# Down projections of three layers turned to stationary tokens and Strassen's scheme, with norm roots on GpSimd

## The chip, the cores and the metric

The kernel runs on one core of one Trainium2 chip. The metric is the time of one execution on the device in microseconds (us). All multiplications are done on TensorE in products of 128 x 128 stationary values against up to 512 moving columns; VectorE, ScalarE and GpSimd (POOL in the profile) prepare operands and read results, SyncE (SP) issues the transfers.

## The reference

A decoder trunk of four layers over one residual stream of 256 tokens with 1024 features. Layer i has the token mixer i mod 3: differential attention, block-sparse attention, sliding-window attention with sinks. Each layer ends in a squared-ReLU MLP with 4096 hidden features; a final norm follows. All in float32.

```python
def rms_norm(x, g):
    y = xf * lax.rsqrt(jnp.mean(xf * xf, axis=-1, keepdims=True) + NORM_EPS)
    return (y * g.astype(jnp.float32)).astype(x.dtype)

def sqrelu_mlp(h, w_up, w_down):
    a = jnp.maximum(h @ w_up, 0)
    return (a * a) @ w_down

for i in range(DEPTH):
    a = rms_norm(h, attn_norm_g[i])
    ...
    h = h + y
    h = h + sqrelu_mlp(rms_norm(h, mlp_norm_g[i]), mlp_w_up[i], mlp_w_down[i])
return rms_norm(h, final_norm_g)
```

## The kernel before

**Precision.** Each operand is split into a high part in the fast format fp32r and a low remainder; a product is the sum of three TensorE products (high x high, high x low, low x high). Weights come in pieces of 128 x 2048 floats (1 MB, tile raw): ScalarE writes whi, VectorE subtracts and writes wlo, both in two halves of 1024 columns. There are four raw buffers and three pairs of whi and wlo.

**Residual stream.** It lies in hT0 to hT3 with features on partitions and tokens on columns. A norm multiplies its gain in first: `Normed.part` writes hg, high part on ScalarE and low part on VectorE, which is the operand of the next products. The norm's scale is put in after the products. `Normed.sum` adds up squares in acc; `row` sums acc over partitions with a GpSimd all-reduce (tile rows); `column` picks each token's sum onto its partition with VectorE (tile nx); `factor` takes the inverse root (tile nr) by ten small VectorE steps, except in layer 0, where the sums come by products and GpSimd's power takes the root. The evictions of the mixer's first products p_in (tile qk, or vkq in layer 2) multiply by nr. After them come the rotation (ropea, ropeb), the transposes p_qk and the scores p_s.

**MLP.** `up_proj` makes 4096 hidden features in 16 groups g of 256, with features on partitions: u is the squared ReLU, uu its high and low parts. The MLP norm's scale is the square of a root, so it's a reciprocal without a root, and it comes behind the down projection. In layers 0 to 2 `down_proj` holds the weights stationary: 8 blocks d of 128 output features, each with 32 blocks of hidden features, a 512-column product with whi (uu's high and low parts side by side) and a 256-column one with wlo, 512 in all. Each pair of blocks is evicted (cross, y), scaled by a row of factors and added to hT.

In layer 3 `down_out` holds the tokens stationary (uu's 128 tokens) and streams 512 output features of the weights. The first 1024 hidden features (g 0 to 3) go by Strassen's scheme with a Winograd form: tokens, hidden features and output features are each halved, and seven products of sums replace eight. `Sums` makes the sums of u in `up_proj`, `Form` and `less` the sums of the weights. Seven `strassen` steps of 4 x 3 products and twelve `plain` pieces of 24 follow one another; results gather in PSUM banks (sums, products p, p_last, p_end), `shared` adds what Strassen's products share. There the result has tokens on partitions, as the output wants it.

**Order.** `Plan` places all tasks: a list scheduler runs a model of the engines forth and back, with a cost written beside each task, and keeps the best of eight orders; EARLIER moves single tasks by hand, by their number (plan.named). The order of instructions on each engine's queue is then fixed, and each queue runs in order: an instruction that waits holds up all behind it.

Of the kernel before, what the change touches and what calls it, by code (L numbers as in the profile page):

```python
# [11 lines left out]
F32 = mybir.dt.float32  # L12
# [31 lines left out]
           4306: -5.2, 4309: -1.1, 4443: -7.1, 6437: -126, 6439: -126}  # L44
# [171 lines left out]
def trunk(ctx: ExitStack, tc: tile.TileContext, xT, gains, lams, swa_row, fng, weights, out):  # L216
# [291 lines left out]
    def rsqrt(y, x, n):  # L508

        t = tiny.tile([P, n], F32, tag="nw", name="nw", bufs=6)  # L510
        V.tensor_scalar(y.bitcast(I32), x.bitcast(I32), -0.5, 1597463007.0, op0=OP.mult, op1=OP.add)
        for _ in range(3):
            V.tensor_tensor(t, y, y, op=OP.mult)
            V.scalar_tensor_tensor(t, t, -0.5, x, op0=OP.mult, op1=OP.mult)
            V.scalar_tensor_tensor(y, t, 1.5, y, op0=OP.add, op1=OP.mult)

    norms = iter(range(100))

    class Normed:
# [704 lines left out]
    def up_proj(n, then, forms=None):  # L1224

        us, pair, read, done, used = [], {}, [None, None], [], {}
        for g in range(16):
# [40 lines left out]
            if forms is not None and g < 4:  # L1268
# [17 lines left out]

    def down_proj(us, n, row):

        def into(j, p, last, begin):

            st = {}

            def to():
                st["y"] = sb.tile([P, 512], F32, tag="y", name="y")
                return r3(2)(st["y"])

            def scaled():
                V.tensor_tensor(r3(2)(st["y"]), r3(2)(st["y"]), row[0][:, None, :].to_broadcast([P, 2, S]), op=OP.mult)
                V.tensor_tensor(hT[j], st["y"], hT[j], op=OP.add)

            a = joined(to, p, [last])
            s = dve(1024, scaled, [a, row[1]], 0.2)
            n.part(2 * j, [s])
            n.part(2 * j + 1, [s])
            n.sum(j, [s])
            give("acc", [a], begin)

        for d in range(8):
            if d % 2 == 0:
                st = {}  # L1310
            for h in range(2):
                w = piece()
                for part, k in ((part, k) for part in ((0, 1), (1, 0))[h] for k in range(16)):

                    def do(d=d, h=h, k=k, part=part, w=w, st=st):
                        if not st:
                            st["p"] = two_banks("p_down")
                        block_step(st["p"][:, d % 2], w.at(part, 16, k), us[16 * h + k][1](), part,
                                   h + k + part == 0, h == 1 and part == 0 and k == 15)

                    at = d % 2 + h + k + part
                    t = product(STEPS[part], do, [us[16 * h + k][0], w.ready(part, 16, k)], {"acc": 1} if at == 0 else None)
                    begin = t if at == 0 else begin
                release(w)
            if d % 2:
                into(d // 2, lambda st=st: st["p"], t, begin)
# [26 lines left out]
    def down_out(us, factor, forms):  # L1353

        st = {}
        res = stream_by_tokens()
        ss = cst.tile([P, NT, 4], F32, name="fss")
        x = cst.tile([P, NT], F32, name="fx")
        r = cst.tile([P, NT], F32, name="fr")
        last = []  # L1360

        def load():
# [355 lines left out]
```

## Time and profile before

| | us |
|---|---|
| median of 3 runs | 1121.19 (1121.08 to 1121.8) |
| the profiled execution's own time | 1121.43 |
| its span, first to last instruction | 1119.3 |
| TensorE busy | 1111.6 (99%) |
| VectorE busy | 845.1 (75%) |
| ScalarE busy | 695.8 (62%) |
| GpSimd busy | 62.7 (6%) |

Rows of the profile read thus: a chain's row is start, duration, engine and tile; a timeline's row is start, duration, engine, operation, output tile, arrow, inputs, and in brackets the idle time ahead of it with what ended it. Almost every instruction carries line 209, that of the helper which issues it, so tiles are named instead. PE is TensorE, PEld its weight loads, DVE VectorE, ACT ScalarE.

### The profile page before, as it was taken

To read this page: it belongs to the slowest core of one execution; us is meant where nothing else is said; L and a number is where in the kernel's file an instruction comes from. 1 tells how busy PE (TensorE), PEld (TensorE's weight loads), DVE (VectorE), ACT (ScalarE), POOL (GpSimd) and SP (SyncE) were. 2 spreads that over 40 slices of the span, in tenths; PEclk is the share of its full clock that TensorE was granted. 3 is DMA by queue.
4 is the path that set the end of the run, shared out by engine and by line. 5 is a ranking of instruction groups with operands and counts; after the bars stand their busy time and mean duration, and the time that the engine had idled before them with its cause. 6 is when DMAs were issued, how large, how long until landed. Compare 5 with 4: busy or idle time off the path is not lost.

```text
span 1119.3 us, 16680 instructions
## 1 busy us (share of the span) xinstructions
PE 1111.6 (99%) x6438; PEld 974.2 (87%) x6438; DVE 845.1 (75%) x1406; ACT 695.8 (62%) x1231; POOL 62.7 (6%) x109
## 2 busy tenths in 40 slices
PE   9999999999999999999999999999999999999997
PEld 7889888888888898888888898888888889888886
DVE  6996987646697678775569898865568787988847
ACT  6996655444497765554357965554448785655693
POOL 4110000000100000000001100000010110000000
PEclk9999999999999999999999999999999999999999
DMA  9545455555444455555553265555544445553740
GB/s 326 174 151 189 173 201 184 196 188 189 150 153 149 155 184 199 177 204 177 206 191 118 76 253 195 181 195 188 189 151 141 172 146 194 188 193 114 282 172 37
DMA packets 30462, 198.63 MB, mean 177 GB/s; under 512 B 3504, under 2 KB 4784, under 8 KB 7216
## 3 DMA queue, kind: packets, MB, share of 16 engines
q1 hardware_dynamic: 30096, 197.35, 50.3%
q8 instruction: 50, 0.82, 0.3%
q10 hardware_dynamic: 288, 0.23, 0.1%
q14 instruction: 28, 0.23, 0.1%
HBM read 196.52 MB, written 1.05 MB: 177 GB/s over the span
## 4 chain that ended last, share of the span: by engine, by line
PE 99%; DMA 0%; DVE 0%; issue 0%; POOL 0%; POOLq 0%; ACT 0%; SPq 0%; DVEq 0%
PE p_up L209 32%; PE p_down L209 24%; PE p_in L209 20%; PE p_d L209 8%; PE p_last L209 4%; PE p L209 3%; PE p_s L209 2%; PE p_av L209 2%; PE p_t L209 1%; PE p_qk L209 1%; PE p_o L209 0%; DMA hT<-in_xT 0%; DVE res L209 0%; POOL fr L209 0%; POOLq L1714 0%
## 5 line engine op out<-in xcount | busy, mean ns | idle before, releaser
L209 DVE TENSOR_TENSOR wlo<-raw,whi 128x1024 fp32r<-128x1024 f32 (+1 forms) x382 | 449.7, 1210 | 187.7 <-ACT whi L209 182.8
L209 ACT ACTIVATE whi<-raw 128x1024 fp32r<-128x1024 f32 (+1 forms) x382 | 380.1, 1038 | 221.1 <-issue 80.0
L209 PE MATMUL p_up<-hg,whi 128*128 128x512 f32 x1024 | 239.9, 390 | 0.0
L209 PEld LDWEIGHTS p_up<-hg,whi 128*128 128x128 f32 x1024 | 189.5, 188 | 38.1 <-DVE hg L209 0.6
L209 PE MATMUL p_in<-whi,hg 128*128 128x512 f32 (+1 forms) x672 | 187.7, 393 | 0.4 <-DVE hg L209 0.4
L209 PE MATMUL p_down<-uu,whi 128*128 128x512 f32 x768 | 179.1, 390 | 0.0
L209 PEld LDWEIGHTS p_down<-uu,whi 128*128 128x128 f32 x768 | 142.7, 188 | 28.6
L209 PEld LDWEIGHTS p_in<-whi,hg 128*128 128x128 f32 x672 | 122.2, 189 | 23.2 <-ACT whi L209 0.9
L209 PEld LDWEIGHTS p_up<-hg,wlo 128*128 128x128 f32 x1024 | 127.6, 192 | 2.8
L209 PE MATMUL p_up<-hg,wlo 128*128 128x256 f32 x1024 | 128.5, 283 | 0.0
L209 PE MATMUL p_in<-wlo,hg 128*128 128x512 f32 (+1 forms) x336 | 106.2, 393 | 0.0
L209 PEld LDWEIGHTS p_down<-uu,wlo 128*128 128x128 f32 x768 | 95.3, 192 | 1.9
L209 PE MATMUL p_down<-uu,wlo 128*128 128x256 f32 x768 | 95.9, 283 | 0.0
L209 PE MATMUL p_d<-oo,whi 128*128 128x256 f32 x512 | 94.9, 286 | 0.0
L209 ACT ACTIVATE uu<-u 128x512 fp32r<-128x512 f32 (+1 forms) x64 | 39.7, 620 | 79.5 <-DVE u L209 79.5
L209 PEld LDWEIGHTS p_d<-oo,whi 128*128 128x128 f32 x512 | 79.6, 191 | 1.1 <-issue 0.9
L209 PE MATMUL p_d<-oo,wlo 128*128 128x256 f32 x256 | 72.4, 283 | 0.0
L209 PEld LDWEIGHTS p_in<-wlo,hg 128*128 128x128 f32 x336 | 61.8, 189 | 11.8 <-DVE wlo L209 0.4
L209 ACT ACTIVATE e<-ns,nm 128x128 f32<-128x128 f32 (+3 forms) x128 | 56.9, 447 | 4.9 <-DVE nm L209 3.8
L209 ACT ACTIVATE cross<-p_up 128x512 f32<-128x512 f32 x64 | 37.7, 590 | 34.6 <-PE p_up L209 34.5
L209 DVE TENSOR_TENSOR relu<-p_up,cross 128x512 f32<-128x512 f32 x64 | 44.0, 688 | 14.0 <-ACT cross L209 13.9
L209 DVE TENSOR_TENSOR uu<-u,uu 128x512 fp32r<-128x512 f32 (+1 forms) x64 | 43.5, 680 | 13.3 <-ACT uu L209 12.6
(200 smaller groups left out, 1110.9 us busy)
## 6 DMA issues: line engine op xcount, KB each, us to landing
raw<-in_weights SPq DMA_DIRECT2D x181, 1024.0 KB, 4.9
raw<-in_weights SPq DMA_DIRECT2D x12, 256.0 KB, 5.0
hT<-in_xT SPq DMA_DIRECT2D x8, 128.0 KB, 4.4
raw<-in_weights SPq DMA_DIRECT2D x2, 512.0 KB, 6.7
bias<-in_swa_row SPq DMA_DIRECT2D x1, 512.0 KB, 6.8
grow<-in_fng SPq DMA_DIRECT2D x1, 512.0 KB, 5.3
out<-last SPq DMA_DIRECT2D x1, 512.0 KB, 2.7
out<-last SPq DMA_DIRECT2D x1, 320.0 KB, 2.6
```

Source lines behind the costliest of these rows:

```text
L209: x = getattr(self.engine, name)(*args, **kw)
```

## The change

The down projections of layers 0 to 2 now take the same path as that of layer 3 (`down_out` becomes `down_proj` for all), with the tokens stationary and Strassen's scheme on the hidden groups g 0 to 3. `up_proj` makes the sums in all layers, the weights are laid out accordingly (16 pieces per layer as before), and the MLP norm's factor is a column (a value per token on its partition) in place of a row. Since the residual stream of these layers has features on partitions, the result is turned back: y0 and y1 take the scaled results, one tile for each half of the tokens; the new function `back` mixes the banks in (mixed), transposes 128 x 128 blocks on TensorE into a bank p_y (turned_back) and adds these to hT (added), for each half c of the output features. The last bank is taken in two halves. `rsqrt` goes, and GpSimd's power takes the root of all mixer norms. The numbers of the tasks are set at each layer's start, so that EARLIER names the tasks it did.

The core of the diff (left out: the bodies of the removed functions, the weight layout, tile declarations, hand-overs of names):

```diff
-           4306: -5.2, 4309: -1.1, 4443: -7.1, 6437: -126, 6439: -126}
+           4306: -5.2, 4309: -1.1, 4443: -7.1, 6439: -126, 6441: -126}
...
-    def rsqrt(y, x, n):
...
         def factor(self, by_products):
             x, a = self.column_by_products() if by_products else self.column()
-            if by_products:
-                return add("POOL", 0.8, lambda: G.tensor_tensor(self.r, x, minus_half[:, :NT], op=OP.pow), [a])
-            return dve(0, lambda: rsqrt(self.r, x, NT), [a], 1.8)
+            return add("POOL", 0.8, lambda: G.tensor_tensor(self.r, x, minus_half[:, :NT], op=OP.pow), [a])
...
                 if g % 2 == 0:
+                    plan.named += 2
                     then(g)
...
-    def down_proj(us, n, row):
...
-    def down_out(us, factor, forms):
+    def down_proj(us, factor, forms, n=None):
+        st, last, res, loaded = {}, [], ([], None), None
+        if n is None:
...
             if c and last:
-                steps = [(0, k, 0, 512) for k in range(4)] + [(1, k, x, x + S) for x in (0, S) for k in range(4)]
+                halves = ((0, 512),) if n else ((0, S), (S, 512))
+                steps = [(0, k, 0, 512) for k in range(4)] + [(1, k, x, y) for x, y in halves for k in range(4)]
...
+                if n:
+                    res[0].extend(room(16 + t, [P, D], f"y{t}") for t in range(NT))
...
+                def do():
+                    o, by = res[0][t][:, 512 * c:512 * c + 512], factor[0][:, t:t + 1]
+                    if n:
+                        V.tensor_scalar(o, x[y], by, None, op0=OP.mult)
+                    else:
+                        V.scalar_tensor_tensor(o, x[y], by, o, op0=OP.mult, op1=OP.add)
...
+            give("acc", [c], begin[6])
...
+            if n:
+                back(c, ends, ready, n, begin, sums, res[0], factor[0])
+                continue
...
+    def back(c, ends, ready, n, begin, sums, y, factor):
+        banks = {}
+        def mixed(t, lo, hi, after):
+            def do():
+                o = y[t][:, 512 * c + lo:512 * c + hi]
+                V.scalar_tensor_tensor(o, sums[((2, 4), (3, 8))[c][t]][:, lo:hi], factor[:, t:t + 1], o, op0=OP.mult, op1=OP.add)
+            return dve(hi - lo, do, [*ready, *after], 0.15, named=False)
+        def turned_back(t, js, after, new):
+            def do():
+                if new:
+                    banks[t] = bank("p_y")
+                for j in js:
+                    for b in range(2):
+                        at = S * (j % 2) + P * b
+                        transpose(banks[t][:, at:at + P], y[t][:, S * j + P * b:S * j + P * b + P])
+            return pe(0.225 * len(js), do, after, take={"wk": 1} if new else None, named=False)
+        def added(t, j, after):
+            def do():
+                o = hT[j].rearrange("p (b t m) -> p b t m", b=2, t=NT)[:, :, t]
+                V.tensor_tensor(o, r3(2)(banks[t][:, S * (j % 2):S * (j % 2) + S]), o, op=OP.add)
+            return dve(256, do, after, named=False)
+        def finished(j, after):
+            n.part(2 * j, after)
+            n.part(2 * j + 1, after)
+            n.sum(j, after)
+        js = (2 * c, 2 * c + 1)
+        if c == 0:
+            both = [mixed(t, 0, 512, [ends[-1][-1]]) for t in range(NT)]
+            give("acc", both, begin[2])
+            turns = [turned_back(t, js, [both[t]], True) for t in range(NT)]
+            adds = [[added(t, j, [turns[t]]) for j in js] for t in range(NT)]
+        else:
+            first = mixed(0, 0, 512, [ends[0][-1]])
+            give("wk", [first], begin[3])
+            turns = [turned_back(0, js, [first], True)]
+            adds = [[added(0, j, [turns[0]]) for j in js], []]
+            rest = [mixed(1, x, x + S, [ends[1][-1]]) for x in (0, S)]
+            give("wk", rest, begin[8])
+            z = None
+            for i in range(2):
+                z = turned_back(1, js[i:i + 1], [rest[i], z], i == 0)
+                turns += [z] * (i == 0)
+                adds[1].append(added(1, js[i], [z]))
+        for t in range(NT):
+            give("wk", adds[t], turns[t])
+        for i, j in enumerate(js):
+            finished(j, [adds[0][i], adds[1][i]])
 
...
-            if g == 2 and i + 1 < DEPTH:
-                s = n.row()
-                def do(n=n):
-                    V.tensor_scalar(row, n.s, 1.0 / D, EPS, op0=OP.mult, op1=OP.add)
-                    V.reciprocal(row, row)
-                held["row"] = (row, dve(1700, do, [s], 0.15))
-            elif g == 2:
-                factor = cst.tile([P, NT], F32, name="factor")
-                other = cst.tile([P, 1], F32, name="other")
+            if g == 2:
+                factor = cst.tile([P, NT], F32, name=f"factor{i}")
                 x, a = n.column()
                 held["factor"] = (factor, dve(0, lambda: V.reciprocal(factor, x), [a]))
...
-        forms = [] if i + 1 == DEPTH else None
+        forms = []
         us = up_proj(n, then, forms)
-        if i + 1 < DEPTH:
-            n = Normed(gv[:, 0, i + 1, :])
-            down_proj(us, n, held["row"])
-        else:
-            down_out(us, held["factor"], forms)
+        n = Normed(gv[:, 0, i + 1, :]) if i + 1 < DEPTH else None
+        down_proj(us, held["factor"], forms, n)
...
```

What the order of instructions shows, at three places between layer 0 and layer 1.

GpSimd's queue before, from the MLP norm's all-reduce of layer 0 (first rows) over the first mixer norm's (second rows), to the next MLP norm's. ISA without operands is an instruction that the compiler puts in where GpSimd goes from one kind of instruction to another:

```order
L209 ISA
L209 ISA rows<-acc_1495 128x256
L209 MEMSET kpad 64x2x256 x2
L209 ISA rows<-acc_2522 128x256
L209 CAST qhl<-qh 64x2x256 x6
L209 ISA rows<-acc_4173 128x256
```

and after:

```order
L209 ISA
L209 ISA rows<-acc_1497 128x256
L209 MEMSET kpad 64x2x256 x2
L209 ISA rows<-acc_2731 128x256
L209 ISA
L209 TENSOR_TENSOR nr_138<-nx_137,minus_half 128x2
L209 CAST qhl<-qh 64x2x256 x8
L209 ISA
L209 ISA rows<-acc_4112 128x256
```

Between the mixer norm's all-reduce and the casts of q there now stand a bare ISA row and the power; another bare row stands ahead of the next all-reduce. The same holds at the starts of layers 2 and 3.

TensorE's queue at the same boundary before, from the end of the down projection:

```order
L209 MATMUL p_down<-uu,whi_2843 128x512 x16
L209 MATMUL p_in<-whi_2890,hg_2515 128x512 x4
L209 MATMUL p_in<-wlo_2891,hg_2515 128x512 x2
L209 MATMUL p_in<-whi_2890,hg_2515 128x512 x4
L209 MATMUL p_in<-wlo_2891,hg_2515 128x512 x2
```

and, after twelve more rows of p_in, up to the transposes of q and k:

```order
L209 MATMUL p_in<-whi_2980,hg_2515 128x512 x4
L209 MATMUL p_in<-wlo_2981,hg_2515 128x512 x2
L209 MATMUL p_in<-whi_2980,hg_2515 128x512 x4
L209 MATMUL p_in<-wlo_2981,hg_2515 128x512 x2
L209 MATMUL p_in<-whi_2980,hg_2689 128x512 x2
L209 MATMUL p_qk<-ident,qk 128x128 x8
```

After, TensorE's queue from the end of the down projection (p_2682 is the bank of the second half of the tokens):

```order
L209 MATMUL p_2682<-whi_2806,uu 128x512
L209 MATMUL p_in<-whi_2838,hg_2717 128x512 x4
L209 MATMUL p_y<-ident,y_2369 128x128 x2
L209 MATMUL p_in<-wlo_2839,hg_2717 128x512
L209 MATMUL p_y<-ident,y_2369 128x128 x2
L209 MATMUL p_in<-wlo_2839,hg_2717 128x512
```

and, after fourteen more rows of p_in, up to the same transposes:

```order
L209 MATMUL p_in<-whi_2914,hg_2717 128x512 x4
L209 MATMUL p_in<-wlo_2915,hg_2717 128x512 x2
L209 MATMUL p_in<-whi_2914,hg_2717 128x512 x4
L209 MATMUL p_in<-wlo_2915,hg_2717 128x512 x2
L209 MATMUL p_in<-whi_2914,hg_2725 128x512
L209 MATMUL p_qk<-ident,qk 128x128 x8
```

The last four turning products stand between the first p_in products of the next layer; p_qk stands behind 61 p_in products and these four, where it stood behind 62.

VectorE's queue there before (y, hT and acc of the last 256 features):

```order
L209 TENSOR_TENSOR y<-p_down,cross 128x512
L209 TENSOR_TENSOR y<-y,row 128x512
L209 TENSOR_TENSOR hT_70<-y,hT_70 128x512
L209 TENSOR_TENSOR wlo_2981<-raw_2822,whi_2980 128x1024
L209 TENSOR_TENSOR acc_2522<-acc_2522,sq 128x512
L209 TENSOR_TENSOR acc_2522<-acc_2522 128x256
```

and after:

```order
L209 SCALAR_TENSOR_TENSOR y_2369<-p_2682,factor_136,y_2369 128x256 x2
L209 TENSOR_TENSOR hT_69<-p_y,hT_69 128x2x128
L209 TENSOR_TENSOR hT_70<-p_y,hT_70 128x2x128
L209 TENSOR_TENSOR wlo_2915<-raw_2795,whi_2914 128x1024
L209 TENSOR_TENSOR acc_2731<-acc_2731,sq 128x512
L209 SCALAR_TENSOR_TENSOR hg_2939<-hT_69,gn,hg_2939 128x256 x2
L209 TENSOR_TENSOR acc_2731<-acc_2731,sq 128x512
L209 TENSOR_TENSOR acc_2731<-acc_2731 128x256
```

Both of the last two hT tiles (hT_69 and hT_70) now end behind the last products, and two low parts of hg stand ahead of the last sums of squares.

More of the change, by code (lines that the diff above doesn't have):

```diff
@@ L504, in lambdas @@
         return dve(0, last, [a], 0.4, rank=4)
-    def rsqrt(y, x, n):
[L510 to L515, printed above, removed]
     norms = iter(range(100))
@@ L1285, in up_proj @@
         return us
-    def down_proj(us, n, row):
[L1289 to L1326, printed above, removed]
     def stream_by_tokens():
@@ L1351, in stream_by_tokens, with load @@
         return res, last
-    def down_out(us, factor, forms):
[L1355 to L1362, printed above, removed]
-            last.extend(sb.tile([P, D], F32, tag=f"hg{t}", name=f"last{t}", bufs=1) for t in range(NT))
-            st["grow"] = sb.tile([P, D], F32, tag="hg2", name="grow", bufs=1)
-            nc.sync.dma_start(st["grow"], bcast(fng, D))
-        loaded = add("DMA", 1.0, load, [factor[1], res[1]], lag=2.0)
+    def down_proj(us, factor, forms, n=None):
+        st, last, res, loaded = {}, [], ([], None), None
+        if n is None:
+            res = stream_by_tokens()
+            ss = cst.tile([P, NT, 4], F32, name="fss")
+            x = cst.tile([P, NT], F32, name="fx")
+            r = cst.tile([P, NT], F32, name="fr")
+            def load():
+                last.extend(sb.tile([P, D], F32, tag=f"hg{t}", name=f"last{t}", bufs=1) for t in range(NT))
+                st["grow"] = sb.tile([P, D], F32, tag="hg2", name="grow", bufs=1)
+                nc.sync.dma_start(st["grow"], bcast(fng, D))
+            loaded = add("DMA", 1.0, load, [factor[1], res[1]], lag=2.0)
         squares, gained, ends_of = {0: [], 1: []}, {0: [], 1: []}, {}
@@ L1512, in plain @@
             if c and last:
-                steps = [(0, k, 0, 512) for k in range(4)] + [(1, k, x, x + S) for x in (0, S) for k in range(4)]
+                halves = ((0, 512),) if n else ((0, S), (S, 512))
+                steps = [(0, k, 0, 512) for k in range(4)] + [(1, k, x, y) for x, y in halves for k in range(4)]
             for t, k, lo, hi in steps:
-                apart, x = c and last and t, ((2, 4), (3, 8))[c][t]
+                apart, x = c and last and t and not n, ((2, 4), (3, 8))[c][t]
                 new = k == 0 if apart else start(x)
@@ L1575, in down_out @@
         plain(early[3], 0, 5, False)
+        before_end = None
         for c in range(2):
@@ L1578, in down_out @@
                 ends = plain(piece(), c, q, q == 7)
-                if c and q == 6:
+                if c and q == 6 and not n:
                     before_end = gathered(1, lambda: sums[8], z)
+            if n:
+                back(c, ends, ready, n, begin, sums, res[0], factor[0])
+                continue
             for t, lo, hi, end in ends:
@@ L1590, in trunk @@
     made = {}
-    row = cst.tile([P, S], F32, name="row")
     n = Normed(gv[:, 0, 0, :])
     for i in range(DEPTH):
+        plan.named = (0, 2032, 3996, 5764)[i]
         parts = mixer_layer(i, n)
@@ L1673, in weight_pieces @@
             rows(up[:, 256 * g:256 * g + 256])
-        if i + 1 < DEPTH:
-            for d in range(8):
-                for h in range(2):
-                    rows(down[2048 * h:2048 * h + 2048, P * d:P * d + P])
-        else:
-            a, b = (np.concatenate([down[x:x + 256], down[x + 512:x + 768]]) for x in (0, 256))
-            at = [down[512 * q:512 * q + 512, 512 * c:512 * c + 512] for c in range(2) for q in range(2, 8)]
-            for w in (a[:, :512], a[:, 512:], at[0], b[:, 512:], at[1], b[:, :512], *at[2:]):
-                rows(w)
+        a, b = (np.concatenate([down[x:x + 256], down[x + 512:x + 768]]) for x in (0, 256))
+        at = [down[512 * q:512 * q + 512, 512 * c:512 * c + 512] for c in range(2) for q in range(2, 8)]
+        for w in (a[:, :512], a[:, 512:], at[0], b[:, 512:], at[1], b[:, :512], *at[2:]):
+            rows(w)
     return out
```

17 lines of the change are left out of this document (9 added, 8 removed).

## The prediction

> **What bounds the kernel now.** I read the page, the waits of TensorE, the chain that ended last, and then the stretches of single layers. First the page (span, busy time, chain by line) and the whole answer on what TensorE waited for:
>
> ```profile
> span 1119.3 us, 16680 instructions
> PE 1111.6 (99%) x6438; PEld 974.2 (87%) x6438; DVE 845.1 (75%) x1406; ACT 695.8 (62%) x1231; POOL 62.7 (6%) x109
> PE p_warm L209 <- DVE minus_half L209: 1.1, 1, 1.1
> PE p_in L209 <- DVE hg L209: 0.4, 1, 0.4
> ```
>
> TensorE waits 1.5 us in all, both times in the first microseconds. So a microsecond of products taken out is a microsecond gained, and a wait put into TensorE's queue is lost in full: no other wait is there to swallow it. The profiled execution took 1121.43 us, 2.1 us beside its span, and stands 0.24 us over the median of 1121.19.
>
> The chain, in order of time, prices the products. The layers 0 to 2 have the old down projection, layer 3 already has the new scheme:
>
> ```profile
> 5.29 14.41 PE p_in L209 x57
> 204.90 88.91 PE p_down L209 x512
> 293.81 14.06 PE p_in L209 x62
> 307.87 0.87 PE p_qk L209 x8
> 581.91 13.87 PE p_in L209 x73
> 595.79 0.66 PE p_qk L209 x6
> 1080.32 29.93 PE p L209 x132
> ```
>
> An old down projection is 512 products in 88.91 us. A 512-column product in layer 3 takes 29.93 / 132 = 0.2267 us, and so does p_in behind the first down projection (14.06 / 62). A transposing product takes 0.87 / 8 = 0.109 us.
>
> Busy time by stretch (span, then PE, PEld, DVE, ACT, POOL): the down projection of layer 0, and the up and down projections of layer 3:
>
> ```profile
> 204.90:293.80 88.90, 88.90 (x514) 78.74 (x513) 49.21 (x52) 38.60 (x46) 1.04 (x2) 1.00 0.56 196
> 939.60:1028.60 89.00, 89.00 (x514) 78.80 (x513) 79.35 (x109) 52.83 (x76) 2.73 (x2) 1.00 0.50 175
> 1028.60:1110.30 81.70, 81.70 (x362) 67.59 (x362) 59.94 (x64) 57.63 (x107) 0.00 (x0) 1.00 0.45 161
> ```
>
> Layer 3 keeps TensorE busy through both stretches, with the sums and weight forms that the other layers now get.
>
> **The products.** New: Strassen 7 x 4 x 3 = 84, plain 12 x 24 = 288, together 372 x 0.2267 = 84.3 us; 16 transposes, 16 x 0.109 = 1.7 us. That is 86.1 against 88.9, or 2.8 us a layer and 8.5 us in three layers. Left alone, this gives 1121.4 - 8.5 = 1112.9.
>
> **What VectorE, ScalarE and the queues get.** Per layer three more weight splits and eight differences of halves:
>
> ```profile
> L209 DVE TENSOR_TENSOR raw<-raw,raw 128x1024 f32<-128x1024 f32 x8 | 9.4, 1220 | 0.0
> L209 ACT ACTIVATE whi<-raw 128x1024 fp32r<-128x1024 f32 (+1 forms) x382 | 380.1, 1038 | 221.1 <-issue 80.0
> ```
>
> VectorE: 8 x 1.22 + 6 x 1.21 = 17 us; ScalarE: 6 x 1.04 = 6 us; the sums of u, part of them in the up stretch, come on top. I cost all of this at nothing: layer 3 carries the same at 59.94 of 81.70 us and 79.35 of 89.00 us of VectorE and also moves its residuals on ScalarE, which the other layers don't. The weight loads stay 16 pieces of 1 MB a layer on SP's queue, in layer 3's order; nothing is added there.
>
> **The layer boundary.** Call T the time when the next layer's p_in starts (293.81 before). TensorE next stops for data at p_qk, which needs the normed and rotated q and k, and these need the norm's root. Rows of the boundary before, and of the two half-width evictions in layer 3's tail, which are the new ones' nearest kin:
>
> ```profile
> L209 DVE SCALAR_TENSOR_TENSOR res<-p_end,factor,res x2: 483/484/484, 1111.7 to 1113.1; 128x256 f32<-128x256 f32 x2
> 297.67 0.68 DVE L209 TENSOR_TENSOR acc<-acc,sq 128x512 f32<-128x512 f32 x1
> 298.39 0.42 DVE L209 TENSOR_TENSOR acc<-acc 128x256 f32<-128x256 f32 x1
> 298.73 1.71 DVE L209 SCALAR_TENSOR_TENSOR hg<-hT,gn,hg 128x256 fp32r<-128x256 f32 x2
> 298.99 1.87 POOL L209 PARTITION_ALL_REDUCE rows<-acc  x1 [6.29 <-DVE acc L209]
> 300.37 1.21 DVE L209 TENSOR_TENSOR wlo<-raw,whi 128x1024 fp32r<-128x1024 f32 x1
> 301.50 0.41 DVE L209 TENSOR_TENSOR rows<-rows,ident 128x256 f32<-128x256 f32 x1
> 302.40 0.17 DVE L209 TENSOR_SCALAR nx<-nx 128x2 f32<-128x2 f32 x1
> 302.60 0.17 DVE L209 TENSOR_SCALAR nr<-nx 128x2 int32<-128x2 int32 x1
> 304.37 0.16 DVE L209 SCALAR_TENSOR_TENSOR nr<-nw,nr 128x2 f32<-128x2 f32 x1
> 304.73 1.27 ACT L209 ACTIVATE qk<-p_in,nr 128x512 f32<-128x512 f32 x2 [3.83 <-PE p_in L209]
> 306.03 0.43 DVE L209 TENSOR_TENSOR ropea<-qk,cc 128x256 f32<-128x256 f32 x1 [0.32 <-ACT qk L209]
> 306.89 0.42 DVE L209 TENSOR_TENSOR qk<-ropea,ropeb 128x256 f32<-128x256 f32 x1
> ```
>
> Before, the root is done at T + 10.7, the evictions start at T + 10.9, when p_in ends, the rotation ends at T + 13.5, and p_qk runs at T + 14.06 without a wait. There is half a microsecond of slack.
>
> After, from the order of instructions: two half evictions, 0.2 + 2 x 0.48 = T + 1.2; second half's turns and sum into hT, T + 2.2; half a weight split 1.21, a sum of squares 0.68, two low halves of hg at about 0.5 each, the last sums 0.68 + 0.42: all-reduce starts at T + 6.3 and ends at T + 8.2. The column (0.41 + 0.42 + 0.17, behind two lows and half a split) is ready at T + 9.5. hg's last parts are ready by about T + 7.4 and are wanted at T + 8.6 and T + 10.0, so TensorE doesn't wait for them. With the power following at once, the root is there by T + 10.6, evictions run to T + 12.7, the rotation to T + 14.0, and p_qk stands at 61 x 0.2267 + 0.44 = T + 14.3. No wait. Taking the ten small VectorE steps away (302.60 to 304.5, 1.9 us) thus pays nothing by itself.
>
> **The bare row on POOL.** The order shows what the diff doesn't: between this all-reduce and the power stands an instruction without operands, as at each place where POOL changes between the two kinds; before, none stood there in layers 1 and 2. I call its time L. It has no row of its own. What the trace has is what came behind such an instruction:
>
> ```profile
> 1.46 0.29 POOL masks.py:199 TENSOR_SCALAR_AFFINE_SELECT ident<-ident 128x128 f32<-128x128 f32 x1 [0.30 <-POOL ident masks.py:197]
> 875.41 1.06 POOL L209 TENSOR_TENSOR ry<-ss,minus_half 128x4 f32<-128x4 f32 x1 [14.20 <-DVE ss L209]
> 989.97 2.14 POOL L209 PARTITION_ALL_REDUCE rows<-acc  x1 [69.53 <-DVE acc L209]
> 1002.37 0.60 POOL L209 TENSOR_TENSOR other<-factor,minus_half 128x1 f32<-128x1 f32 x1 [10.27 <-DVE factor L209]
> ```
>
> Lower end: at the kernel's start such an instruction fits into a gap of 0.30 us. Upper end: in layer 3 all-reduce, bare row and power follow each other as they will now; the all-reduce ends at 992.11 and the power starts at 1002.37, so L is 10.26 at most (the wait is put down to VectorE, which proves no more than that L isn't longer). I take L = 7.0, two thirds of the way up, since the upper row has the same engine and the same change of kind and the start may have changed nothing. With it the power starts at T + 8.2 + L, takes 1.0 (as ry), and evictions, rotation and hand-overs add 1.27 + 1.22 + 0.4: p_qk can run at T + 12.05 + L. In layers 1 and 3 it stands at T + 14.3: TensorE waits L - 2.25. Queued behind on POOL are the casts of q, which wait for p_qk anyway; on ScalarE the weight split behind the evictions, wanted ten microseconds later.
>
> Layer 2 evicts on VectorE and rotates fewer columns:
>
> ```profile
> 592.83 1.41 DVE L209 SCALAR_TENSOR_TENSOR vkq<-p_in,nr,bias 128x512 f32<-128x512 f32 x2 [0.18 <-PE p_in L209]
> 595.01 0.36 DVE L209 TENSOR_TENSOR vkq<-ropea,ropeb 128x192 f32<-128x192 f32 x1
> ```
>
> From 592.83 to 595.37 is 2.54 us, so the same sum; p_qk stands behind 48 x 0.2267 + 0.44 + 29 half-width products at (13.87 - 10.88) / 25 = 0.12: T + 14.8, a wait of L - 2.75. Three boundaries: 3L - 7.25. Against 8.5 us of products the change loses as soon as L passes 5.2 us. **The sum** with L = 7.0: 1121.4 - 8.5 + 13.8 = 1126.7, or 1126.5 against the median. Its ends are 1112.9 (L under 2.25) and 1136.5 (L = 10.26).
>
> The Trainium skill ("GPSIMD Engine Reference", the path of an instruction) says that Q7 kernels are loadable, and that the first call after such a load pays about 6 us that no instruction of a profile shows. By it, as an estimate, the sum would be 1123.7; the trace allows that (0.30 to 10.26) and shows nothing nearer.
>
> **Rivals.**
> - The bare row is hidden (the other side). It costs under 2.3 us, or nothing as at 1.46 us; the column on VectorE then ends last, TensorE doesn't wait, and the time is about 1113. The gap of 0.30 us and an unchanged power behind it (1.06 against 1.0) speak for it; that ry's instruction had 14.2 us to hide in speaks against reading much into that. It decides at L = 5.2.
> - A middling or near-break-even price, L of 5.5 to 6.5: 1122 to 1125. The skill's page named above is this case.
> - The wait also slows TensorE after it. At the start the first 57 p_in took 14.41 us, 1.49 us more than 57 x 0.2267, after 0.4 us of waiting behind a slow warm-up. If each of the three waits ended so: 1126.5 + 4.5 = 1131; with L near 10 up to 1140. The trace has no long wait later on that would show it, and a granted clock of 1.00 in each stretch above. The Trainium skill ("TensorE: Matmul & The Clock Gate", Part 1) has the clock go to half after an idle window of about 3.4 us; no run here shows it.
> - The turned-back sums come late: if half a weight split (1.21 us) stands before each eviction, TensorE waits about 1 us at each boundary, 3 us more.
>
> **How the numbers follow.** Forecast, L from 6.5 to 9: 1125 to 1133, 0.32. L near 6: 1121.5 to 1125, 0.16, half of it within 0.2% (2.2 us, about what a measurement can tell). L near 10 or slow restarts: 1133 to 1140, 0.12. Hidden: 1112 to 1115.5, 0.30. Between hidden and break-even: 1115.5 to 1121, 0.10, a third of it within 0.2%. So faster 0.37, same 0.10, slower 0.53. The range that leaves out little but the third case is 1112 to 1134; the forecast's own is 1125 to 1133.
>
> **What would show it.** Products: the chain has 84.3 us for each down stretch and 16 p_y of 0.109. Boundary: the all-reduce of layers 1 to 3 starts 6.3 us after p_in's start. Bare row: the gap from the end of that all-reduce to the start of nr<-nx is L + 0; if it is 1.3 us, where the column ends, the forecast is wrong and the hidden case right. Wait: TensorE idles before p_qk by L - 2.25, released by the rotation; p_in right behind tells whether the rate drops. Covers: waits of p_up, p or p_last on weight splits would mean that VectorE's 17 us were not free.

## The result and the profile after

The changed kernel takes 1132.22 us (median of 4 runs, 1129.19 to 1132.8), the kernel before 1121.49 on the same chip (1121.08 to 1121.92): a ratio of 1.009 with an interval of 1.0071 to 1.0109. It is 10.7 us slower, where 5.3 were forecast (1126.5 against 1121.19): the right sign, a time inside the range, and twice the size. The profiled execution took 1132.8 us, with a span of 1131.0.

The page's busy times, and the whole answer on what TensorE waited for, of the changed kernel:

```profile
PE 1110.5 (98%) x6066; PEld 956.2 (85%) x6066; DVE 903.4 (80%) x1498; ACT 717.2 (63%) x1265; POOL 63.2 (6%) x112
PE p_qk L209 <- DVE qk L209: 7.8, 2, 4.0
PE p_qk L209 <- DVE vkq L209: 4.1, 1, 4.1
PE p_warm L209 <- DVE minus_half L209: 1.1, 1, 1.1
PE p_y L209 <- DVE hT L209: 0.8, 3, 0.3
PE p_in L209 <- DVE hg L209: 0.4, 1, 0.4
```

Three waits of 4 us stand before the first p_qk of layers 1 to 3 (two end on qk, layer 2's on vkq); there were none. They are 11.9 us, and TensorE has 372 instructions fewer, yet its busy time fell by only 1.1 us (1111.6 to 1110.5): part of its work runs slower than before. The chain in order of time shows where. Around each boundary, with the first p_in behind p_qk (310.95, 603.69, 855.87):

```profile
115.90 1.16 PE p_up L209 x5
290.69 0.91 PE p_in L209 x4
310.95 4.64 PE p_in L209 x15
407.98 2.03 PE p_up L209 x9
582.74 0.93 PE p_in L209 x4
603.69 4.67 PE p_in L209 x23
661.43 2.61 PE p_up L209 x14
836.17 0.94 PE p_in L209 x4
855.87 5.03 PE p_in L209 x15
951.38 3.72 PE p_up L209 x20
```

From p_up's start to the next p_in's start lies a layer's MLP, from there to the next p_up its mixer. The same points of the chain before, and the differences:

| us | layer boundary 0/1 | 1/2 | 2/3 | sum |
|---|---|---|---|---|
| MLP before | 177.92 | 177.91 | 177.92 | |
| MLP after | 174.79 | 174.76 | 174.74 | -9.5 |
| mixer behind it, before | 110.19 | 71.20 | 108.60 | |
| mixer behind it, after | 117.29 | 78.69 | 115.21 | +21.2 |

So the products gained 9.5 us, the three mixers lost 21.2, and -9.5 + 21.2 is the 11.7 us by which the span grew. Of the mixers' 21.2 us, 1.3 are turning products that fall behind p_in's start (3 x 0.44), 0.8 the waits on hT, 11.9 the waits before p_qk. Of the 7.2 us that are left, 5.8 are TensorE's clock; the other 1.4 aren't broken down here. Stretches of 3 us from the start of each of the three p_qk (span, then PE, PEld, DVE, ACT, POOL busy, then the granted clock, DMA share, GB/s):

```profile
309.46:312.46 3.00, 3.00 (x13) 2.61 (x14) 2.60 (x4) 2.45 (x5) 1.21 (x2) 0.58 0.00 0
312.46:315.46 3.00, 3.00 (x13) 2.41 (x12) 2.49 (x4) 2.23 (x4) 0.00 (x0) 0.85 0.00 0
315.46:318.46 3.00, 3.00 (x20) 2.65 (x19) 2.97 (x7) 1.34 (x4) 0.00 (x0) 1.00 0.74 254
602.15:605.15 3.00, 3.00 (x14) 3.00 (x15) 2.50 (x4) 2.07 (x5) 0.63 (x2) 0.50 0.01 3
605.15:608.15 3.00, 3.00 (x17) 2.87 (x16) 1.49 (x4) 0.92 (x1) 0.90 (x3) 0.71 0.03 5
854.81:857.81 3.00, 3.00 (x14) 2.57 (x15) 2.65 (x4) 2.71 (x5) 1.22 (x2) 0.71 0.01 3
857.81:860.81 3.00, 3.00 (x11) 2.38 (x11) 2.32 (x3) 1.97 (x4) 0.00 (x0) 0.72 0.01 3
```

TensorE is busy all the time in them, at a clock of 0.50 to 0.85 (means over 3 us) for 6 us; then it is back at 1.00. What is missing there of full rate is 3 x (0.42 + 0.15) = 1.7 us, 3 x (0.50 + 0.29) = 2.4 and 3 x (0.29 + 0.28) = 1.7, together 5.8 us.

The cause of the waits is on POOL. Its rows at the three boundaries of the changed kernel:

```profile
297.00 1.87 POOL L209 PARTITION_ALL_REDUCE rows<-acc  x1 [19.23 <-DVE acc L209]
305.96 0.73 POOL L209 TENSOR_TENSOR nr<-nx,minus_half 128x2 f32<-128x2 f32 x1 [7.09 <-issue]
589.07 1.87 POOL L209 PARTITION_ALL_REDUCE rows<-acc  x1 [19.25 <-DVE acc L209]
598.80 0.73 POOL L209 TENSOR_TENSOR nr<-nx,minus_half 128x2 f32<-128x2 f32 x1 [7.85 <-issue]
842.51 1.87 POOL L209 PARTITION_ALL_REDUCE rows<-acc  x1 [19.25 <-DVE acc L209]
851.31 0.73 POOL L209 TENSOR_TENSOR nr<-nx,minus_half 128x2 f32<-128x2 f32 x1 [6.93 <-issue]
```

Between the all-reduce's end and the power lie 6.93 to 7.85 us of idle time that the profile gives to nothing ("issue"): the operand-less row's L. The trace names that row: in layer 1 it is a MODIFY_POOL_CONFIG, recorded twice, at 298.82 and 298.86 us, for 0.09 us each; behind it POOL has no record until the power at 305.96.

### The profile page after: what moved, and what is told of

The parts are those of the page before. It is cut to its first block, busy times and chain, and to the rows that moved or that the text cites. A ratio compares the mean times of both kernels' runs of the same rounds, so it can differ in the third digit from the quotient of the medians.

```text
span 1131.0 us, 16065 instructions
## 1 busy us (share of the span) xinstructions
PE 1110.5 (98%) x6066; PEld 956.2 (85%) x6066; DVE 903.4 (80%) x1498; ACT 717.2 (63%) x1265; POOL 63.2 (6%) x112
## 4 chain that ended last, share of the span: by engine, by line
PE 95%; DVE 2%; issue 1%; DMA 0%; POOL 0%; ACT 0%; POOLq 0%; SPq 0%; DVEq 0%
PE p_up L209 31%; PE p_in L209 18%; PE p_last L209 15%; PE p L209 14%; PE p_d L209 8%; PE p_s L209 2%; PE p_av L209 2%; PE p_t L209 1%; PE p_qk L209 1%; DVE wlo L209 1%; PE p_y L209 1%; DVE hg L209 0%; PE p_o L209 0%; DVE acc L209 0%; DMA hT<-in_xT 0%
## 5 line engine op out<-in xcount | busy, mean ns | idle before, releaser
L209 DVE TENSOR_TENSOR wlo<-raw,whi 128x1024 fp32r<-128x1024 f32 (+1 forms) x400 | 469.0, 1204 | 120.4 <-ACT whi L209 119.0
L209 ACT ACTIVATE whi<-raw 128x1024 fp32r<-128x1024 f32 (+1 forms) x400 | 398.8, 1040 | 187.3 <-PE p_last L209 51.2
L209 PE MATMUL p_in<-whi,hg 128*128 128x512 f32 (+1 forms) x672 | 190.2, 398 | 0.4 <-DVE hg L209 0.4
L209 PEld LDWEIGHTS p_in<-whi,hg 128*128 128x128 f32 x672 | 124.8, 193 | 23.8 <-ACT whi L209 0.7
L209 PE MATMUL p_last<-whi,uu 128*128 128x512 f32 x448 | 139.8, 389 | 0.0
L209 PE MATMUL p<-whi,uu 128*128 128x512 f32 x440 | 139.1, 391 | 0.0
L209 PEld LDWEIGHTS p_last<-whi,uu 128*128 128x128 f32 x448 | 84.1, 188 | 17.3
L209 PEld LDWEIGHTS p<-whi,uu 128*128 128x128 f32 x440 | 82.6, 188 | 17.0
L209 PE MATMUL p_last<-wlo,uu 128*128 128x512 f32 x224 | 87.1, 389 | 0.0
L209 PE MATMUL p<-wlo,uu 128*128 128x512 f32 x220 | 85.6, 389 | 0.0
L209 PEld LDWEIGHTS p_in<-wlo,hg 128*128 128x128 f32 x336 | 63.2, 193 | 11.6 <-DVE wlo L209 0.2
```

The lines of the kernel that those rows point to most:

```text
L209: x = getattr(self.engine, name)(*args, **kw)
```

## The experiments

My theory A: POOL's stop L makes the three waits, and the waits make the low clock; without both, the new products pay. Rivals: B, the new order with the turned-back sums is itself the slower one and the wait only covers that; D, what is slow behind the wait is late data, not the clock; E, POOL stops behind an all-reduce for any instruction, not for the power alone. Each kernel was timed beside the kernel before on its chip.

### VectorE's root put back

The change with before's ten VectorE steps for the root; the planner counts them at 1.8 us on VectorE, as before.

```diff
-            return add("POOL", 0.8, lambda: G.tensor_tensor(self.r, x, minus_half[:, :NT], op=OP.pow), [a])
+            if by_products:
+                return add("POOL", 0.8, lambda: G.tensor_tensor(self.r, x, minus_half[:, :NT], op=OP.pow), [a])
+            return dve(0, lambda: rsqrt(self.r, x, NT), [a], 1.8)
```

> The changed kernel with the ten small VectorE steps for the root of the mixer norms again, so that no bare row and no power stand behind the all-reduce at the starts of layers 1 to 3. Theory A (the loss is the wait for GpSimd's change of kind, and TensorE's slower clock behind that wait): the down projections keep their 9.5 us, the mixers give back all but the 0.44 us of transposes and some 0.3 us of small waits each, so 1113 to 1115, below both kernels. Rival B (the loss comes from the turning back: the sums into hT come later at the boundary and VectorE is fuller): the mixers keep most of their 21 us, so 1125 to 1132.

Measured: 1120.98 us, ratio 0.9992 (0.9983 to 1.0002), no difference from before, between the two expectations. The boundary did what A says: no wait stands before the first p_qk of layers 1 to 3. But another wait came up, in layer 2's mixer:

```profile
PE p_t L209 <- ACT e L209: 1.8, 1, 1.8
PE p_t L209 <- DVE et L209: 0.4, 1, 0.4
```

With another cost in the plan the whole order came out differently: layer 2's mixer took 76.67 us, 5.5 over before, with these waits among its heads and a granted clock of 0.72 in the 6 us around them. This run changes two things at once (the root and the order), and so decides nothing alone.

### The kernel before with POOL's power

Only the root moves to POOL; the old down projections stay.

```diff
-            if by_products:
-                return add("POOL", 0.8, lambda: G.tensor_tensor(self.r, x, minus_half[:, :NT], op=OP.pow), [a])
-            return dve(0, lambda: rsqrt(self.r, x, NT), [a], 1.8)
+            return add("POOL", 0.8, lambda: G.tensor_tensor(self.r, x, minus_half[:, :NT], op=OP.pow), [a])
```

> The kernel before with one edit: GpSimd's power takes the root of all mixer norms. Its all-reduce ends 7.05 us after p_in's start; with a change of kind of 6.9 to 7.9 us, a power of 0.73 and 2.8 us to p_qk, TensorE can go on at 17.5 to 18.4 us where it stood at 14.06. Theory A: a wait of 3.5 to 4.4 us and some 2 us of slow clock at each of three boundaries, 17 to 19 us more, so 1138 to 1141. Rival B: the root isn't the matter, 1121 to 1123.

Measured: 1137.82 us, ratio 1.0146 (1.0129 to 1.0163), 0.2 us under A's range. The power alone costs 16.1 us without any of the new products. Its gaps on POOL are 7.78, 6.70 and 7.37 us, its waits before p_qk:

```profile
PE p_qk L209 <- DVE qk L209: 8.6, 2, 4.5
PE p_qk L209 <- DVE vkq L209: 3.0, 1, 3.0
```

These 11.6 us leave 4.9 of the 16.5 us by which its span grew (1119.3 to 1135.8): again more than the waits. Two of the three waits lower the clock, those of layers 1 and 3 (4.52 and 4.10 us; 0.50 and 0.65 in the 3 us behind them, 0.50 and 0.78 in the next 3). That is 4.7 us of full rate. Behind layer 2's wait of 3.00 us the clock stays at 1.00.

### The all-reduce taken out instead

The change with the norm's sums made by TensorE's products, as in layer 0, so that POOL has no all-reduce directly ahead of the power.

```diff
-        r = n.factor(False) if i else None
+        r = n.factor(True) if i else None
+        plan.named += i > 0
```

> The changed kernel with the mixer norms' sums by TensorE products, as layer 0 has them (p_sum, four products, 0.44 us a layer), and GpSimd's power kept. The change of kind then stands behind the MLP norm's all-reduce, some 100 us ahead of the power that needs it. Theory A: no wait before p_qk, so 1114 to 1116 (the root on VectorE plus 1.3 us at most, or less since the root comes earlier). Rival C (the power itself, or any use of GpSimd in the chain of the norm, is what is slow): 1125 or more. Rival B: 1125 to 1132.

Measured: 1117.41 us, ratio 0.9962 (0.9949 to 0.9975), a little above the expected range and faster than both kernels. No 4 us wait is left (0.3 us in all before p_qk), and the power is still POOL's. The MODIFY_POOL_CONFIG now stands behind the MLP norm's all-reduce and a memset (at 277.96 us, 20 us ahead of the power at 298.31), so its stop is over when the power is due. So neither the power nor the new products need make TensorE wait; the power right behind the all-reduce does. The order of the other tasks changed too in this run, so its time alone doesn't price the stop.

### The wait filled with idle products

The change with 32 products of ones into p_qk's own bank ahead of the first p_qk, so that TensorE does not stand still.

```diff
+            for _ in range(fill):
+                matmul(st["p"][:, :P], ones, ones, True, True)
...
+        made["fill"] = 32 if i else 0
```

> The changed kernel with 32 idle products (128 columns of ones, into p_qk's own bank ahead of its transposes) at the starts of layers 1 to 3: about 3.5 us of work in the wait of about 4.0 us, which adds nothing to the result. Theory A with the clock as a term of its own: p_qk starts no earlier, but the 15 to 23 p_in behind it run at 0.2267 us again, 6 us less than the changed kernel, so 1125 to 1127. Rival D (the slow products behind the wait come of late operands and not of the clock, or the granted clock falls for another reason): 1131 to 1133.

Measured: 1136.37 us, ratio 1.0133 (1.0118 to 1.0148), a miss: each idle product is two records of 0.114 us, so the filling took twice what I had counted and pushed p_qk back. TensorE's rows:

```profile
305.08 7.30 PE L209 MATMUL p_qk<-ones 128*128 128x128 f32 x64
312.22 1.04 PE L209 MATMUL p_qk<-ident,qk 128*128 128x128 f32 x8
```

Counted from p_in's start, p_qk stands 3.0, 2.9 and 3.2 us later than in the changed kernel, 9.1 us in the three layers, but the span grew by only 3.3 (1131.0 to 1134.3). The difference of 5.8 us is what the low clock cost, and the clock is 1.00 behind each p_qk here. This spoke for the clock and called for a filling of the right length.

### The changed order, VectorE's root

The planner still counts a POOL step of 0.8 us, so TensorE's order is the changed kernel's; only at that step VectorE's rows are issued. POOL has neither power nor operand-less row there.

```diff
-            return add("POOL", 0.8, lambda: G.tensor_tensor(self.r, x, minus_half[:, :NT], op=OP.pow), [a])
+            if by_products:
+                return add("POOL", 0.8, lambda: G.tensor_tensor(self.r, x, minus_half[:, :NT], op=OP.pow), [a])
+            return add("POOL", 0.8, lambda: rsqrt(self.r, x, NT), [a])
```

> The changed kernel with its planned order kept row for row on TensorE (the planner still counts a POOL step of 0.8 us), but at that step VectorE issues before's rows for the root instead of POOL's power. Theory A (POOL's stop between all-reduce and power, and TensorE's lowered clock behind the waits, are the whole loss at the boundary): the column's root is there about 1.5 us after the sum, the waits before p_qk (11.9 us in three layers) and the slow rows behind them (6 us) are gone, the mixers fall back to 111 to 112, 72 to 73 and 109 to 110 us, and the time is 1114 to 1116 us, faster than the kernel before. Theory B (the order itself, with transposes p_y on TensorE's path and VectorE loaded by 17 us more a layer, costs the mixers their time, and the wait only hides it): 1121 us or more, no faster than the kernel before.

Measured: 1119.05 us, ratio 0.9979 (0.9969 to 0.9988): faster than before, so B falls, but 3 us above what A gave. Against the changed kernel the span is 13.9 us shorter (1131.0 to 1117.1): 8.6 of waits (11.9 to 3.3) and about 5.8 of clock, which is 1.00 behind all three p_qk (0.5 us more than the difference of the spans, which isn't placed). What A had left out are the 3.3 us still waited:

```profile
PE p_qk L209 <- DVE qk L209: 2.1, 2, 1.2
PE p_qk L209 <- DVE vkq L209: 1.2, 1, 1.2
300.18 0.17 DVE L209 TENSOR_SCALAR nx<-nx 128x2 f32<-128x2 f32 x1
300.29 1.23 DVE L209 TENSOR_TENSOR wlo<-raw,whi 128x1024 fp32r<-128x1024 f32 x1
301.43 0.16 DVE L209 TENSOR_SCALAR nr<-nx 128x2 int32<-128x2 int32 x1
303.19 0.16 DVE L209 SCALAR_TENSOR_TENSOR nr<-nw,nr 128x2 f32<-128x2 f32 x1
```

In this order a weight split of 1.23 us stands between the column (nx) and the ten small rows, which last 1.9 us more. So the removed VectorE steps are hidden only where the order leaves them room; the changed order, made for POOL's root, doesn't.

### A filling of the right length

```diff
-        made["fill"] = 32 if i else 0
+        made["fill"] = 14 if i else 0
```

> The changed kernel with 14 idle products of ones (two passes of 0.228 us each, 6.4 us by the long filling's rows less what overlaps; about 3.2 us where only every second record counts) into p_qk's own bank ahead of the first p_qk of layers 1 to 3, so that TensorE works on until the transposes can start, without pushing them back much. Theory A (the lowered clock is a term of its own, about 2 us a boundary, set off by the idle wait): p_in's rows behind the wait run at full rate, granted clock 1.00 there, and the time is 1125 to 1128 us, 5 to 7 us under the changed kernel. Theory D (the time behind the wait is late data, not clock): the time stays 1131 to 1134 us.

Measured: 1126.78 us, ratio 1.0051 (1.0036 to 1.0066). A right, D falls. The 14 products took 3.29 us, 0.235 each, and not the 6.4 that the expectation also named. TensorE's rows at the first boundary, and the granted clock behind it:

```profile
305.40 3.29 PE L209 MATMUL p_qk<-ones 128*128 128x128 f32 x28
309.31 1.06 PE L209 MATMUL p_qk<-ident,qk 128*128 128x128 f32 x8 [0.62 <-DVE qk L209]
309.31:312.31 3.00, 3.00 (x18) 2.62 (x19) 2.65 (x4) 2.71 (x5) 1.22 (x2) 1.00 0.00 0
312.31:315.31 3.00, 3.00 (x20) 2.68 (x19) 2.94 (x4) 2.65 (x4) 0.00 (x0) 1.00 0.00 0
```

p_qk starts when it did (309.31 against 309.46), the power is as late as before, transfers are as idle as before; only TensorE did worthless work in place of waiting, and 38 rows of TensorE ran in the 6 us where 26 did. Its span is 6.3 us shorter, of which 0.9 are p_qk starts that came earlier by themselves (mostly layer 2's) and 5.4 the clock. This kernel shows the clock as a term of its own.

### How long a wait lowers the clock

The same with 7, and with 3 idle products.

```diff
-        made["fill"] = 14 if i else 0
+        made["fill"] = 7 if i else 0
```

> The changed kernel with 7 idle products ahead of the first p_qk of layers 1 to 3 (0.235 us each by the 28 rows in 3.29 us of the filling with 14): 1.6 us of work, so about 2.3 us of idle time is left of 4.0. If the clock falls by the length of the idle stretch and a wait of 2.3 us is too short for it, the rows behind run at full rate and the time is as with 14, 1125.5 to 1128; if any wait over some 1.2 us (the longest so far without a lowered clock) does it, 1130 to 1133.

> The changed kernel with 3 idle products: 0.7 us of work, about 3.3 us of idle time left. If the length of the stretch decides and its threshold lies near 4, the time is 1125.5 to 1128 and the clock 1.00 behind the wait; if it lies below 3.2, the clock is 0.6 to 0.8 there and the time 1130 to 1133; near the threshold some layers show it and others not, 1127 to 1131.

Measured: 1131.7 us, ratio 1.0088 (1.0073 to 1.0103), with 7, and 1130.63 us, ratio 1.0084 (1.0069 to 1.0099), with 3, where all three waits (3.13, 3.46 and 3.82 us) lowered the clock. For 7 the expected gain for a harmless wait did not come: POOL's gaps came out longer there (8.23 and 8.10 us in layers 2 and 3), so only layer 1's wait was as short as intended. So the answer is read by waits, not by kernels. Two p_qk of the kernel with 7, and one of the kernel before with POOL's power (606.22):

```profile
309.65 1.06 PE L209 MATMUL p_qk<-ident,qk 128*128 128x128 f32 x8 [2.24 <-DVE qk L209]
601.02 0.88 PE L209 MATMUL p_qk<-ident,vkq 128*128 128x128 f32 x6 [2.86 <-DVE vkq L209]
606.22 0.88 PE L209 MATMUL p_qk<-ident,vkq 128*128 128x128 f32 x6 [3.00 <-DVE vkq L209]
```

Over the changed kernel and the two short fillings there are eight such waits of 2.86 to 4.05 us, and behind every one the clock is 0.50 to 0.74 in the first 3 us. Behind the six waits of 0.62 to 2.24 us in the filling with 7, the filling with 14 and the kernel with VectorE's root it is 1.00. But it is 1.00 behind the wait of 3.00 us too, so the length of a wait doesn't decide alone.

A finer cut shows what does. In the traces that have it, the half rate starts and ends on a grid of 3.41 us that doesn't follow the waits: in the changed kernel it starts at 309.95, 600.08 and 856.08 us, which are 85 and 75 steps of 3.413 us apart. Along this grid, the wait of 2.86 us (first two rows) and that of 3.00 us (last three):

```profile
598.73:602.14 3.41, 1.12 (x10) 1.12 (x11) 3.31 (x7) 0.62 (x2) 0.00 (x0) 1.00 0.00 0
602.14:605.55 3.41, 3.41 (x18) 3.41 (x18) 2.22 (x4) 1.72 (x5) 1.52 (x4) 0.50 0.03 7
601.10:604.51 3.41, 2.12 (x18) 1.92 (x16) 0.88 (x2) 0.54 (x1) 0.73 (x1) 1.00 0.92 315
604.51:607.92 3.41, 1.70 (x15) 1.70 (x16) 3.14 (x7) 1.18 (x3) 0.00 (x0) 1.00 0.00 0
607.92:611.34 3.42, 3.42 (x27) 3.20 (x26) 2.92 (x7) 2.82 (x5) 1.53 (x4) 1.00 0.00 0
```

The wait of 2.86 us leaves TensorE idle for 2.29 us of one step (3.41 less 1.12), and the next step runs at 0.50. The wait of 3.00 us is parted into 1.29 and 1.71 us, and the steps behind both run at 1.00. Beyond the program's start, all runs together have twelve steps with 1.94 us or more idle, and the step behind each is at 0.50; behind the steps that ran at full rate with 1.71 us or less idle it is 1.00. Layer 2's wait in the changed kernel idles 1.98 and 2.07 us in two steps running, and the half rate lasts 6.83 us. In the first experiment one step holds 1.96 us of idle time, 1.8 of them a single wait, and half rate follows.

The Trainium skill ("TensorE: Matmul & The Clock Gate", Part 1) has the clock go to half after an idle window of about 3.4 us, on a window that runs freely. The half rate and the freely running 3.41 us agree; that the whole window must be idle does not, since 1.94 us of it were enough here, and the measurement decides. From these numbers, as an estimate, a wait under 1.7 us costs no clock unless other stops fall into the same step, and one of 1.9 to 3.4 us does or doesn't by where it falls; all eight waits over 3.4 us here did.

### The planner told what the power costs

The changed kernel with one number changed; POOL still does all-reduce, operand-less row and power.

```diff
-            return add("POOL", 0.8, lambda: G.tensor_tensor(self.r, x, minus_half[:, :NT], op=OP.pow), [a])
+            return add("POOL", 0.8 if by_products else 8.0, lambda: G.tensor_tensor(self.r, x, minus_half[:, :NT], op=OP.pow), [a])
```

> The changed kernel with the planner told 8.0 us for the power of a mixer's norm in place of 0.8, and nothing else; POOL still takes all-reduce, stop and power. The planner moves p_qk behind more rows of p_in. Theory A (the loss is an order that was planned with 0.8 us for what takes 7.7): the waits of 4 us before p_qk shrink below 1 us, the clock stays at 1.00 behind them, and the time is 1115 to 1122 us; what is late then is the heads that follow the first p_qk. Theory C (the mixer's chain from the norm to the heads is its bound, so that a late root costs its 7 us wherever p_qk stands): 1129 to 1134 us, with the waits moved to p_s, p_t or p_o.

Measured: 1116.53 us, ratio 0.9958 (0.9943 to 0.9973), the fastest here, 15.7 us under the changed kernel and in A's range. POOL's power of layer 1, then the chain at that boundary:

```profile
305.82 0.73 POOL L209 TENSOR_TENSOR nr<-nx,minus_half 128x2 f32<-128x2 f32 x1 [7.12 <-DVE wlo L209]
292.60 18.64 PE p_in L209 x82
311.24 0.87 PE p_qk L209 x8
312.11 3.43 PE p_in L209 x15
```

The gap on POOL is still 7.1 us (this time put down to another engine), and the root comes no earlier. But 82 products of p_in now stand ahead of p_qk behind the last turning products, TensorE waits for nothing before p_qk, and the 15 products behind p_qk take 3.43 us where they took 4.6 to 5.0. The mixers are 1.3, 1.5 and 1.9 us over before's in place of 7.1, 7.5 and 6.6. C falls: p_qk now stands 20.7 us behind p_in's start, 2 us later than in the changed kernel, and that does no harm as long as TensorE has products to do meanwhile.

With 9.0 in place of 8.0:

> The changed kernel with the planner told 9.0 us for the power (8.0 gave 1116.5). If a value a little too long costs nothing, because other rows of p_in stand ahead of p_qk, 1116 to 1118 and no wait over 0.5 us before p_qk; if the later start of the heads costs, 1118 to 1121 with waits at p_t or p_s.

Measured: 1117.14 us, ratio 0.9957 (0.9941 to 0.9974): the same within the intervals, no wait before p_qk. A cost that is a little too high does no harm.

### VectorE's root with its cost told

The kernel with the changed order and VectorE's root, the step counted at 2.5 us in place of 0.8.

```diff
-            return add("POOL", 0.8, lambda: rsqrt(self.r, x, NT), [a])
+            return add("POOL", 2.5, lambda: rsqrt(self.r, x, NT), [a])
```

> As the kernel with the same order and VectorE's root, but the planner counts 2.5 us for the root in place of 0.8. Theory A (what that kernel still lacked, three waits of 1.1 us before p_qk and the heads behind them, comes from a root that the plan counted too short): the waits shrink below 0.3 us and the time falls to 1115 to 1117 us. Theory B (any other plan of this kernel loses elsewhere, as the one with 1.8 us on VectorE did): 1118 to 1122 us, with waits at p_t or p_s.

Measured: 1118.59 us, ratio 0.9975 (0.9964 to 0.9986), with waits of 2.7 us before p_qk still: a miss for A. The time is in B's range, but the waits aren't where B had them, at p_t or p_s. A weight split (1.22 us) again stands between the column and the small rows; that the plan moved p_qk too little because this split isn't in the step's cost is likely, not shown.

### A copy on POOL in place of the power

POOL copies the column, VectorE takes the root of the copy.

```diff
+            def copied_root():
+                xc = tiny.tile([P, NT], F32, tag="nx", name="nx", bufs=2)
+                G.tensor_copy(xc, x)
+                rsqrt(self.r, xc, NT)
+
+            return add("POOL", 0.8, copied_root, [a])
```

> As the kernel with the same order and VectorE's root, but POOL first copies the column (a plain copy of 128x2) to a tile of its own, from which VectorE then takes the root; POOL runs no power in the mixer's norm. Theory A (only the power asks for other code than the all-reduce): the copy runs within 1 us of the all-reduce, no wait before p_qk, 1114 to 1117 us. Theory E (any ordinary row of POOL behind an all-reduce pays the stop): the copy stands 7 us behind the all-reduce, the waits are longer than the changed kernel's by VectorE's rows (about 1.3 us each), and the time is 1133 to 1139 us.

Measured: 1119.27 us, ratio 0.998 (0.9971 to 0.999), as with VectorE's root alone, with 3.8 us of waits before p_qk where that kernel has 3.3; above A's range for the reason given there. E falls by POOL's rows:

```profile
296.62 1.87 POOL L209 PARTITION_ALL_REDUCE rows<-acc  x1 [19.25 <-DVE acc L209]
300.27 1.14 POOL L209 COPY nx<-nx 128x2 f32<-128x2 f32 x1 [1.78 <-DVE nx L209]
```

The copy runs 0.06 us after its operand (nx, ready at 300.21), 1.78 us behind the all-reduce (not within 1 us, as A had it, because the operand came that late), and the trace has no MODIFY_POOL_CONFIG between them. Of the two operations tried behind the all-reduce, only the power has it and pays for it; others weren't tried.

## Why the forecast fell short

- **Products**: right. 85.8 us for each down stretch against 86.1 forecast and 88.9 before; with the turning products that fall behind p_in, 8.2 us gained against 8.5.
- **Covers**: right. VectorE carries 58 us more and ScalarE 21, and no wait of p_up, p or p_last on a weight split appears.
- **Start of the all-reduce**: right, 6.3 us behind p_in's start in layers 1 to 3, as forecast.
- **L**: right, and in part by luck, since 7.0 was chosen between bounds of 0.30 and 10.26 with no row nearer. 7.09, 7.85 and 6.93 were measured; over the 24 boundaries of the eight kernels that have the pair, 6.7 to 8.3. The Trainium skill's page on GpSimd, "GPSIMD Engine Reference" (2.1 Instruction dispatch), has about 6 us with no visible instruction: the trace's empty stretch behind MODIFY_POOL_CONFIG agrees in kind, and the size is 0.7 to 2.3 us more here. What POOL does in it no run shows.
- **Waits**: 11.9 in place of 13.8. p_qk could start about 0.4 us sooner than at T + 12.05 + L, since the power takes 0.73 and not 1.0, and it stood about 0.5 us later in its queue, of which 0.3 are waits of p_y on hT. That half microsecond, three times, is lost too (1.6 us). Its 0.8 us of p_y waits are the rival of late turned-back sums at a quarter of its price; the rest isn't broken down.
- **What failed: the sum stopped at the end of the waits.** It priced p_in behind a wait at full rate and put the slow restart among the rivals, at 1.5 us each, inside a chance of 0.12, since no trace showed one. It is 5.8 us, 1.7 to 2.4 a wait, and came with every wait the sum itself forecast, so it was no rival of the forecast but a part of it. The first 57 p_in of the program, 1.49 us too slow, was the nearest row for its price (the trace shows no lowered clock there), and the rule of the clock gate cited beside it named the condition: the forecast waits of 4.3 to 4.8 us were past its 3.4. That the time still fell between 1125 and 1133 is luck: this range was left wide for an L up to 9, and with the measured L the forecast's own sum gives 1112.9 + 21.87 - 7.25 = 1127.5. The rival's own sum, 1131, came nearest.
- Put together: 1126.7 + 0.35 (products) - 1.9 (waits) + 1.6 (p_qk's place) + 5.8 (clock) = 1132.5, against 1132.8 of the profiled execution. The last 0.3 us I can't place.
- **A step that the forecast lacked**: why L turns into a wait at all. The plan counts the power at 0.8 us and sets p_qk right where the root would then be there. With 8.0 us in its place the same L makes no wait before p_qk, so the loss of 10.7 us is one of order, not of work.

What stays open: why L varies from 6.7 to 8.3 us between boundaries and runs, and what idle time between 1.71 and 1.94 us in a step does to the clock. The mixers of the fastest kernel are still 4.7 us over before's in sum; 2.1 of these are p_y's products and waits, the rest isn't broken down.

## What to carry to other kernels

A price that a scheduler doesn't know becomes a stall at the place where it trusts the old one: find the late row, give the plan its measured cost, and try that before taking the change back. When a forecast puts a wait of 3 us or more on TensorE, add some 2 us for the lowered clock behind it, in the sum and not among the rivals: here ten of eleven such waits (2.86 to 4.52 us) lowered it, for 1.7 us of lost rate or more in the changed kernel. Two operations that each run freely on an engine can cost 7 us as neighbours; look at the order of instructions for rows without operands, and at what could hide them.

## What the runs showed of the hardware

In the mixers' norms a power on GpSimd behind an all-reduce starts 6.7 to 8.3 us after it, with a MODIFY_POOL_CONFIG of 0.09 us recorded in between; a plain copy there has neither (1.78 us behind, with its operand 0.06 us old). TensorE's granted clock falls to 0.50 for a step of 3.41 us, on a fixed grid, when TensorE idled for 1.94 us or more of the step before, and stays at 1.00 with 1.71 us or less. So a wait of 3.00 us parted by the grid did nothing, and one of 2.86 us lowered the clock. Worthless products of ones in three such waits kept it at 1.00 and so took 5.4 us off the time. A 128 x 128 product of plain float32 is two records of 0.114 us each.
